# Moving the last up group of block two behind block four's out-projection, and giving the token forms other tiles

## The chip, the cores and the metric

One core of one Trainium2 chip runs the kernel: TensorE (PE) multiplies matrices into PSUM, VectorE (DVE) and ScalarE (ACT) compute between SBUF and PSUM, GpSimd (POOL) and SyncE (SP) issue DMAs here, POOL also small steps. The metric is the device time of one execution in microseconds, the median of several runs.

## The reference, cut to what matters

```python
# h: 2064 tokens x 1024 (16 meta tokens, then 2048), all float32
hn = rms_norm(h, g_mix); proj = hn @ w_in            # q, k, v and the Fourier input u
attn = block_attention(rope(q), rope(k), v)          # 4 heads, 2 key/value heads
four = fourier_mix(u, w_f)
h = h + concat(rms_norm(attn), rms_norm(four)) @ w_out
m = rms_norm(h, g_mlp)
h = h + jnp.square(jax.nn.relu(m @ w_up)) @ w_down   # 1024 -> 4096 -> 1024
return rms_norm(h, g_final)[:, N_META:]
```

The change lies between the end of attention and the end of the MLP.

## The kernel before

Products in float32 are made of three matmuls (`mm3`, lines 71 to 76): each operand is split into a high part (an ACT copy to fp32r, line 64) and a low part (a DVE subtraction, line 65).

The 2048 tokens form four blocks of 512, each with four row tiles of 128. Attention is a generator of steps (`attention`, line 662: 32 units of ten steps), run inside the MLP of earlier blocks: `mix` (line 883) advances another generator and, after each piece of it, attention to a share of its steps. `out_a(b)` (line 906) is the out-projection of block b, `up` and `down` (lines 965, 994) are one group of 512 hidden columns of the MLP: `up` leaves relu-squared activations, split, and `down` multiplies them with the down weights in two halves of the output columns. Weights come through `wtile` (line 874): three raw tiles `wr`, four `wh`, four `wl`.

Blocks one and two (b = 0, 1) run this MLP. `head(0)` and `head(1)` (line 1043) are mixed with attention (lines 1070 to 1075). In `head(1)` all groups but the last are done, up and down. Then, without attention, come `up(1, 7)`, `out_a(3)`, and `down(1, 7)`.

Blocks three and four share their MLP as one product of 1024 tokens by Strassen-Winograd, with seven products in the order "1265734" per group of columns (line 1088). `flip` (line 1128) transposes the normed rows of a block on PE and ACT into `b11`, `b21` (block three, read back from DRAM into `h2`) and `b12`, `b22` (block four). `b_form` (line 1149) splits one of the seven token forms, computed from these by `minus` (line 1178), into `bf` tiles. `up_weights` (line 1095) loads 1024 KB blocks `R0`, `R1` of the up weights and splits the seven weight forms, four ahead. The products go to PSUM banks `ux` and `uy`, from which ACT and DVE make copies `p` and results `c`, `s`; the results go out to DRAM (`s_d`). Tiles of a new pool take the places of tiles of released pools, and each may be written as soon as the tiles that had its place are done (`reuse_waits="tile"`).

The order in program text: `down(1, 7)` half 0 with the flips between, forms 1 and 2, `down(1, 7)` half 1, `final(1)` (line 1024: the last norm of block two, its rows out), then forms 6, 5, 7, 3 and 4. The program's builder may reorder instructions of an engine within what the data allow.

The down stage (`down_operands`, line 1301) forms both operands of its seven products per group from `s_d` and the down weights. Its first product's operands are made early in the up stage's tiles (`first_down`, line 1218); the weight block `w11`, read there into the place of `R1`, is used again for the first difference `t1` (lines 1343 to 1351). Raw activations have a ring of 6 (`ar`), split ones of 10 (`a`); split weights get their pool `dr` in the place of `sp` (lines 1422 to 1426). In the first group these loads are on POOL's queue, later on SP's.

Of the kernel before, what the change touches and what calls it, by code (L numbers as in the profile page):

```python
# [18 lines left out]
P = 128  # L19
# [110 lines left out]
def encoder_block(ctx: ExitStack, tc: tile.TileContext, x, meta, w_in, w_f,  # L130
# [768 lines left out]

    mp = Lines(tc.alloc_tile_pool(name="mp", bufs=1, reuse_waits="tile"), small)  # L900
# [5 lines left out]
    def out_a(b):  # L906
# [111 lines left out]
    def load_gfin(b):  # L1018
        gfin = [a_tile(f"gfin_{b}_{i}") for i in range(2)]
# [4 lines left out]
    def final(b, early=None):  # L1024

        b0, n = BLOCKS[b]
        hs = H.pop(b)
        gfin = early or load_gfin(b)
        for t in range(2 * n):
# [40 lines left out]
    n0, n1 = 8 + 4 + 8 * 15 + 8, 8 + 8 * 14 + 8  # L1070
# [7 lines left out]
    drain(up(1, 7))  # L1078
# [14 lines left out]
    hm = Lines(tc.alloc_tile_pool(name="hm", bufs=1, side="right", reuse_waits="tile"), small)  # L1093
# [31 lines left out]
    UW = up_weights()  # L1125
    ready = [next(UW) for _ in range(4)]

# [18 lines left out]
    b11, b21 = (ra.tile([P, 4, 512], F32, name=f"b{i}1", tag=f"b{i}1") for i in (1, 2))  # L1146
    BF = {}

    def b_form(name, t, src):
        t = t.rearrange("p l k n -> p (l k) n")  # L1150
        BF[name] = hi, lo = t[:, 0:4], t[:, 4:8]
        for c in (slice(0, 2), slice(2, 4)):
            split(hi[:, c], lo[:, c], src[:, c])

    B = {}

    def flips():
        yield from flip(2, h2, (b11, b21))
        hm.release()
        B["rb"] = rb = Lines(tc.alloc_tile_pool(name="rb", bufs=1, side="right", reuse_waits="tile"), small)  # L1160
        B["b"] = [rb.tile([P, 4, 512], F32, name=f"b{i}2", tag=f"b{i}2") for i in (1, 2, 3)]
        yield from flip(3, H.pop(3), B["b"][:2])
# [8 lines left out]
    b_form("1", ey.tile([P, 2, 4, 512], R32, name="bf1", tag="e0"), b11)  # L1171
    b_form("2", ey.tile([P, 2, 4, 512], R32, name="bf2", tag="e1"), b21)
# [3 lines left out]
    two = (slice(0, 2), slice(2, 4))  # L1176

    def minus(dst, a, b):
        for c in two:
            nc.vector.tensor_tensor(dst[:, c], a[:, c], b[:, c], op=ALU.subtract)  # L1180
# [12 lines left out]
    b_form("3", bt["3"], b22)  # L1193
# [3 lines left out]
    b_form("4", sl4.tile([P, 2, 4, 512], R32, name="bf4", tag="bf4"), b21)  # L1197
# [20 lines left out]
    def first_down():  # L1218
# [15 lines left out]
        yield w  # L1234

    first = first_down()
    for g in range(8):
# [5 lines left out]
        for name in ORDER:  # L1243
            hi, lo = ready.pop(0)
            m = BF[name]
            for p in range(2):
# [6 lines left out]
                for k in range(4):  # L1253
                    mm3(nc, o, (hi[:, k, ps], lo[:, k, ps]), (m[0][:, k], m[1][:, k]),
# [38 lines left out]
    *_, w11 = first  # L1293
    pc.release()
    sl4.release()
    sl.release()
    dn = Lines(tc.alloc_tile_pool(name="dn", bufs=1, reuse_waits="tile"), small)

    RING = {"a": (dn, 10)}

    def down_operands():

        for g in range(4):
# [11 lines left out]
            def stationary(name):  # L1315
                S[name] = []
                for h in range(2):
                    r = dn.tile([P, 2, 512], F32, name=f"a{name}_{g}_{h}", tag="ar", bufs=6)
                    eng = nc.sync if g else nc.gpsimd
                    eng.dma_start(r, s_d[g][:, ORDER.index(name), 2 * h:2 * h + 2])  # L1320
                    S[name].append(r)

            def form(name, src):
                got = []
                for h in range(2):
                    for x, r in (("a", S[name][h]), ("b", src[h])):
                        pool, bufs = RING[x]
                        own = x == "b" and name == "2"
                        hi, lo = (pool.tile([P, 2, 512], R32, name=f"{x}{e}{name}_{g}_{h}",
                                            tag=f"{x}{e}{h}" if own else x, bufs=1 if own else bufs) for e in "hl")  # L1330
# [218 lines left out]
```

## Time and profile before

| | us |
|---|---|
| median of 3 runs | 2378.97 |
| lowest, highest | 2374.52, 2379.42 |
| the profiled execution | 2378.81 |
| its span, first to last instruction | 2377.0 |
| PE busy | 2319.6 (98%) |
| DVE busy | 1751.8 (74%) |
| ACT busy | 1296.6 (55%) |

The profile is of one execution. The stages by time: input projections to about 310, Fourier part with attention to about 600, MLP of blocks one and two with attention to about 1660, the passage described above to 1737, the Strassen up stage to 2053, the down stage to the end. Busy time of PE is modelled at its end, so the time in which PE starts nothing is read from what it waited for.

### The profile page before, as it was taken

To read this page: it belongs to the slowest core of one execution; us is meant where nothing else is said; L and a number is where in the kernel's file an instruction comes from. 1 tells how busy PE (TensorE), PEld (TensorE's weight loads), DVE (VectorE), ACT (ScalarE), POOL (GpSimd) and SP (SyncE) were. 2 spreads that over 40 slices of the span, in tenths; PEclk is the share of its full clock that TensorE was granted. 3 is DMA by queue.
4 is the path that set the end of the run, shared out by engine and by line. 5 is a ranking of instruction groups with operands and counts; after the bars stand their busy time and mean duration, and the time that the engine had idled before them with its cause. 6 is when DMAs were issued, how large, how long until landed. Compare 5 with 4: busy or idle time off the path is not lost.

```text
span 2377.0 us, 33687 instructions
## 1 busy us (share of the span) xinstructions
PE 2319.6 (98%) x12326; PEld 1975.7 (83%) x12326; DVE 1751.8 (74%) x2961; ACT 1296.6 (55%) x2525; POOL 170.2 (7%) x225
## 2 busy tenths in 40 slices
PE   8999999999999999999999999999989999899998
PEld 7889889888788888888878888888868888788886
DVE  5435678998688877787887887887675656687786
ACT  6434355654666656565765665665565555543343
POOL 1212120101100000000000000000000000100000
PEclk9999999999999999999999999999999999999999
DMA  6334152434333222234242434223424444855431
GB/s 210 105 102 117 45 170 53 154 125 143 129 92 115 76 76 70 77 103 118 72 142 76 146 92 129 67 76 111 155 89 168 137 165 155 318 173 169 141 124 71
DMA packets 168534, 288.64 MB, mean 121 GB/s; under 512 B 14144, under 2 KB 63008, under 8 KB 168240
## 3 DMA queue, kind: packets, MB, share of 16 engines
q1 hardware_dynamic: 145968, 246.90, 32.0%
q0 software_dynamic: 22400, 39.59, 6.0%
q8 instruction: 97, 1.59, 0.3%
q14 instruction: 69, 0.57, 0.1%
HBM read 216.93 MB, written 69.50 MB: 121 GB/s over the span
## 4 chain that ended last, share of the span: by engine, by line
PE 75%; DVE 5%; ACT 2%; DMA 2%; issue 1%; POOL 1%; SPq 0%; POOLq 0%; DVEq 0%; ACTq 0%
PE pdn L74 5%; PE pdn L75 5%; PE pdn L76 5%; PE pup L74 4%; PE pup L75 4%; PE pup L76 4%; PE s L74 2%; PE s L76 2%; PE s L75 2%; PE ux L74 2%; PE ux L76 2%; PE ux L75 2%; PE o L757 2%; PE dx L75 2%; PE dx L74 2%; PE dx L76 2%
## 5 line engine op out<-in xcount | busy, mean ns | idle before, releaser
L74 PE MATMUL pdn<-wh_dn,ah 128*128 128x512 f32 x512 | 202.4, 397 | 0.8 <-ACT wh_dn L64 0.7
L74 PE MATMUL pup<-mT,wh_up 128*128 128x512 f32 x512 | 202.0, 396 | 0.6 <-ACT mT L67 0.6
L76 PE MATMUL pup<-mT,wl_up 128*128 128x512 f32 x512 | 202.4, 398 | 0.0
L75 PE MATMUL pup<-mT,wh_up 128*128 128x512 f32 x512 | 202.1, 395 | 0.0
L75 PE MATMUL pdn<-wl_dn,ah 128*128 128x512 f32 x512 | 202.1, 395 | 0.0
L76 PE MATMUL pdn<-wh_dn,al 128*128 128x512 f32 x512 | 199.8, 393 | 0.0
L696 ACT COPY S<-s 128x512 f32<-128x512 f32 (+1 forms) x288 | 159.8, 559 | 60.6 <-PE s L76 42.0
L736 DVE TENSOR_TENSOR S<-S,mb 128x512 f32<-128x512 f32 (+1 forms) x288 | 185.5, 652 | 4.8 <-ACT mb L725 4.7
L741 ACT ACTIVATE S<-S 128x512 f32<-128x512 f32 (+1 forms) x264 | 155.6, 602 | 60.8 <-DVE S L736 59.7
L64 ACT CAST wh_up<-wr_up 128x512 fp32r<-128x512 f32 x128 | 79.3, 620 | 167.7 <-PE pdn L76 71.8
L74 PE MATMUL s<-q,kt 128*128 128x256 f32 (+1 forms) x544 | 158.7, 292 | 1.1 <-ACT S L696 1.1
L703 DVE TENSOR_TENSOR M<-M,S 128x512 f32<-128x512 f32 (+1 forms) x224 | 145.2, 648 | 14.8 <-ACT S L696 13.3
L76 PE MATMUL s<-q,kt 128*128 128x256 f32 (+1 forms) x544 | 154.7, 284 | 0.0
L65 DVE TENSOR_TENSOR wl_up<-wr_up,wh_up 128x512 fp32r<-128x512 f32 x128 | 87.5, 687 | 90.5 <-ACT wh_up L64 90.4
L75 PE MATMUL s<-q,kt 128*128 128x256 f32 (+1 forms) x544 | 154.2, 283 | 0.0
L64 ACT CAST wh_dn<-wr_dn 128x512 fp32r<-128x512 f32 x128 | 79.2, 619 | 100.5 <-PE pdn L76 54.6
L65 DVE TENSOR_TENSOR wl_dn<-wr_dn,wh_dn 128x512 fp32r<-128x512 f32 x128 | 87.8, 686 | 54.9 <-ACT wh_dn L64 54.0
L64 ACT CAST ah<-a 128x1024 fp32r<-128x1024 f32 x56 | 58.6, 1050 | 121.8 <-issue 67.1
L763 DVE TENSOR_TENSOR acc<-acc,S 128x512 f32<-128x512 f32 x168 | 114.9, 684 | 2.2 <-ACT S L741 2.1
L65 DVE TENSOR_TENSOR pl<-S,ph 128x512 fp32r<-128x512 f32 x168 | 114.3, 684 | 2.1 <-ACT ph L64 1.3
L74 PE MATMUL o<-ph,vt 128*128 128x256 f32 x384 | 111.2, 290 | 2.1 <-ACT ph L64 2.0
L74 PEld LDWEIGHTS s<-q,kt 128*128 128x128 f32 (+1 forms) x544 | 102.7, 189 | 11.6 <-ACT S L696 2.3
(311 smaller groups left out, 6814.6 us busy)
## 6 DMA issues: line engine op xcount, KB each, us to landing
wr_up<-in_w_up_dram SPq DMA_DIRECT2D x128, 256.0 KB, 2.8
wr_dn<-in_w_down_dram SPq DMA_DIRECT2D x128, 256.0 KB, 2.7
a<-s_d SPq DMA_DIRECT2D x42, 512.0 KB, 3.6
R<-in_w_up_dram SPq DMA_DIRECT2D x16, 1024.0 KB, 5.6
s_d<-s SPq DMA_DIRECT2D x64, 256.0 KB, 2.1
d<-in_w_down_dram SPq DMA_DIRECT2D x26, 512.0 KB, 4.6
s_d<-c SPq DMA_DIRECT2D x48, 256.0 KB, 2.3
h<-h_d SPq DMA_DIRECT2D x20, 512.0 KB, 5.9
```

The lines of the kernel that those rows point to most:

```text
L64: nc.scalar.copy(hi, src)
L65: nc.vector.tensor_tensor(lo, src, f32v(hi), op=ALU.subtract)
L74: nc.tensor.matmul(out, a[0], b[0], start=first, stop=False, skip_group_check=chain)
L75: nc.tensor.matmul(out, a[0], b[1], start=False, stop=False, skip_group_check=chain)
L76: nc.tensor.matmul(out, a[1], b[0], start=False, stop=last, skip_group_check=chain)
L696: nc.scalar.copy(S[:rows, :n], ps[:rows, :n])
L703: nc.vector.tensor_tensor(M[:rows, :n], M[:rows, :n], S[:rows], op=ALU.max)
L736: nc.vector.tensor_tensor(S, S, bc(s["mb"][:rows], [rows, n, 256]), op=ALU.subtract)
L741: nc.scalar.activation(p, S, AF.Exp, scale=ISQ)
L757: nc.tensor.matmul(s["O"], vt[t // 4][:, t % 4], p[:, e], start=t == 0, stop=False)
L763: nc.vector.tensor_tensor(acc, acc, p, op=ALU.add)
```

## The change

- Attention is spread over `head(1)` without the second last down product; `down(1, 6)` follows when attention has ended, then `out_a(3)`. `up(1, 7)` now comes behind `out_a(3)`, with the flips between its pieces, and both halves of `down(1, 7)` behind it.
- The row tiles `h` get a pool `hp` of their own. `h2` lies in the places of `R0` and `R1`; the up weights start behind the flips. `b12`, `b22` and a third block are there from the start.
- Token forms are lists of tiles: 1 and 2 in `ey` as before, 5 in block four's rows and 7 in block two's (`in_hp`), 6 in the `wh` and `wl` slots (`in_wp`), 3 and 4 in small pools. Form 5 comes between the two down halves, 6 right behind them, ahead of `final(1)`.
- `final(1)` no longer has `gfin` multiplied into the first half beforehand; it loads `gfin` into `wr` slots and does both halves on DVE.
- The copies `p` of the first column half lie in `wr` slots, three each.
- Down stage: the first group loads the block (1, 1) again instead of keeping `w11`; two weight blocks and stationary "6" load behind form 2; form 2 has tiles of its own for both operands; the rings are 8 and 5; `gfin` is loaded first, and squares go to two fixed tiles.

```diff
+    hp = Lines(tc.alloc_tile_pool(name="hp", bufs=1, reuse_waits="tile"), small)
     mp = Lines(tc.alloc_tile_pool(name="mp", bufs=1, reuse_waits="tile"), small)
...
-            h = mp.tile([P, D], F32, name=f"h_{b}_{t}", tag=f"h{int(b == 1)}", bufs=4)
+            h = hp.tile([P, D], F32, name=f"h_{b}_{t}", tag=f"h{int(b == 1)}", bufs=4)
...
-                if early and i == 0:
-                    nc.scalar.activation(v, v, AF.Copy, scale=rs)
-                else:
-                    nc.vector.scalar_tensor_tensor(v, v, rs, gfin[i], op0=ALU.mult, op1=ALU.mult)
+                nc.vector.scalar_tensor_tensor(v, v, rs, gfin[i], op0=ALU.mult, op1=ALU.mult)
...
-            if grp < 7:
+            if grp < 7 - b:
                 yield from down(b, grp)
...
-    n0, n1 = 8 + 4 + 8 * 15 + 8, 8 + 8 * 14 + 8
+    n0, n1 = 8 + 4 + 8 * 15 + 8, 8 + 8 * 13 + 8
...
-    drain(up(1, 7))
+    drain(down(1, 6))
     drain(out_a(3))
...
-    UW = up_weights()
-    ready = [next(UW) for _ in range(4)]
-
     def flip(b, hs, raw):
...
-    for t in range(4):
-        h = hm.tile([P, D], F32, name=f"h2_{t}", tag=f"h2_{t}")
-        nc.sync.dma_start(h, h_d[8 + t])
-        h2.append(h)
+    for i in range(2):
+        h = sp.tile([P, 2, D], F32, name=f"h2_{i}", tag=f"R{i}")
+        for t in range(2):
+            nc.sync.dma_start(h[:, t], h_d[8 + 2 * i + t])
+            h2.append(h[:, t])
...
+    def in_ey(e):
+        t = ey.tile([P, 2, 4, 512], R32, name=f"bf{e}", tag=f"e{e}").rearrange("p l k n -> p (l k) n")
+        return [t[:, 0:2], t[:, 2:4]], [t[:, 4:6], t[:, 6:8]]
+
+    def in_hp(e, name):
+        t = [hp.tile([P, 2, 512], R32, name=f"bf{name}_{i}", tag=f"h{e}", bufs=4) for i in range(4)]
+        return t[:2], t[2:]
+
+    def in_wp(name):
+        return tuple([wp.tile([P, 1, 512], R32, name=f"bf{e}{name}_{i}", tag="w" + e, bufs=4) for i in range(4)]
+                     for e in "hl")
...
-    for _ in down(1, 7, (0,)):
-        next(fl)
+    for _ in up(1, 7):
         next(fl, None)
     drain(fl)
-    rb, (b12, b22, b22t) = B["rb"], B["b"]
-    gfin = load_gfin(1)
...
-    for t in range(4):
-        nc.vector.tensor_tensor(H[1][t][:, :512], H[1][t][:, :512], gfin[0], op=ALU.mult)
-    drain(down(1, 7, (1,)))
...
+    UW = up_weights()
+    ready = [next(UW) for _ in range(4)]
+    b_form("1", in_ey(0), b11)
+    b_form("2", in_ey(1), b21)
+    drain(down(1, 7, (0,)))
     minus(b11, b12, b11)
     minus(b22t, b22, b11)
-    final(1, gfin)
+    b_form("5", in_hp(0, "5"), b11)
+    drain(down(1, 7, (1,)))
+    b_form("6", in_wp("6"), b22t)
     mp.release()
-    wp.release()
     sl = Lines(tc.alloc_tile_pool(name="sl", bufs=1, reuse_waits="tile"), small)
-    bt = {n: sl.tile([P, 2, 4, 512], R32, name="bf" + n, tag="bf" + n) for n in "6573"}
-    b_form("6", bt["6"], b22t)
-    b_form("5", bt["5"], b11)
+    final(1, load_gfin(1, [wp.tile([P, 512], F32, name=f"gfin_1_{i}", tag="wr", bufs=3) for i in range(2)]))
     minus(b12, b22, b12)
-    b_form("7", bt["7"], b12)
-    b_form("3", bt["3"], b22)
+    b_form("7", in_hp(1, "7"), b12)
+    b_form("3", in_pool(sl, "3"), b22)
     minus(b21, b21, b22t)
...
-                    d[p] = pc.tile([P, 512], F32, name=f"p{name}_{nm}", tag="p", bufs=6)
+                    d[p] = (pc if p else wp).tile([P, 512], F32, name=f"p{name}_{nm}", tag="p" if p else "wr", bufs=3)
...
-    RING = {"a": (dn, 10)}
+    RING = {"a": (dn, 8)}
...
-                    r = dn.tile([P, 2, 512], F32, name=f"a{name}_{g}_{h}", tag="ar", bufs=6)
+                    r = dn.tile([P, 2, 512], F32, name=f"a{name}_{g}_{h}", tag="ar", bufs=5)
...
-            else:
-                raw[1, 1] = [w11[:, 0:2], w11[:, 2:4]]
             stationary("2")
             load(2, 1)
-            load(1, 2)
-            load(2, 2)
-            stationary("6")
             if g == 0:
-                t1 = [dn.tile([P, 2, 512], F32, name=f"d11_0_{h}", tag="d11", bufs=2) for h in range(2)]
-                sub(t1, raw[1, 2], raw[1, 1])
+                own2("a")
+                load(1, 1)
+            if g:
+                load(1, 2)
+                load(2, 2)
+                stationary("6")
             yield form("1", raw[1, 1]) if g else FIRST
             yield form("2", raw[2, 1])
-            t3, t4 = raw[1, 2], raw[2, 1]
+            if g == 0:
+                load(1, 2)
+                load(2, 2)
+                stationary("6")
+            t1, t3, t4 = raw[1, 1], raw[1, 2], raw[2, 1]
...
-            if g:
-                t1 = raw[1, 1]
-                sub(t1, raw[1, 2], raw[1, 1])
+            sub(t1, raw[1, 2], raw[1, 1])
             sub(t2, raw[2, 2], t1)
```

## Rows read from the trace of the kernel before

**Rows 1.** The page, busy us, share of the span and instructions by engine.

```profile
PE 2319.6 (98%) x12326; PEld 1975.7 (83%) x12326; DVE 1751.8 (74%) x2961; ACT 1296.6 (55%) x2525; POOL 170.2 (7%) x225
```

**Rows 2.** What PE waited for: us in total, times, longest; whole run.

```profile
PE uy L74 <- ACT bf L64: 7.5, 2, 6.9
PE dy L75 <- DVE bl L65: 6.2, 1, 6.2
...
PE uy L75 <- DVE bf L65: 1.7, 1, 1.7
PE ux L74 <- ACT p L1268: 1.4, 1, 1.4
...
PE pmt L1136 <- DVE h L1132: 0.7, 1, 0.7
PE pdn L74 <- ACT wh_dn L64: 0.7, 1, 0.7
```

**Rows 3.** Stretches: length, then busy us by engine, clock, DMA share, GB/s.

```profile
1746.40:1753.30 6.90, 0.00 (x0) 0.00 (x0) 6.46 (x9) 5.05 (x7) 1.68 (x2) 0.77 0.78 289
1753.30:1760.25 6.95, 5.22 (x11) 3.68 (x12) 6.95 (x7) 5.32 (x6) 0.00 (x0) 0.50 0.50 165
```

**Rows 4.** Timeline of PE: start us, duration, instruction, times; the passage.

```profile
1734.67 0.39 PE L75 MATMUL uy<-bf,wuh 128*128 128x512 f32 x1
1734.90 0.39 PE L76 MATMUL uy<-bf,wul 128*128 128x512 f32 x1
...
1736.71 0.39 PE L76 MATMUL pdn<-wh_dn,al 128*128 128x512 f32 x1
...
1757.26 0.63 PE L74 MATMUL uy<-bf,wuh 128*128 128x512 f32 x1
1757.69 0.63 PE L75 MATMUL uy<-bf,wuh 128*128 128x512 f32 x1
```

**Rows 5.** Stretches as in rows 3, start of the down stage.

```profile
2053.00:2065.00 12.00, 12.00 (x54) 9.62 (x52) 4.96 (x8) 4.06 (x5) 0.00 (x0) 1.00 1.04 406
...
2071.30:2075.00 3.70, 3.70 (x10) 2.94 (x11) 3.70 (x4) 3.24 (x4) 0.08 (x1) 0.58 0.00 0
```

**Rows 6.** Groups by line and shape, 1703.3 to 1790: busy us, mean ns; idle before.

```profile
L65 DVE TENSOR_TENSOR bf<-b,bf 128x1024 fp32r<-128x1024 f32 x14 | 16.1, 1219 | 7.7 <-ACT bf L64 7.7
...
L1136 PE MATMUL pmt<-ident,h 128*128 128x128 f32 x64 | 9.0, 277 | 0.7 <-DVE h L1132 0.7
...
L1132 DVE TENSOR_SCALAR h<-h,rs_m 128x1024 f32<-128x1024 f32 x8 | 5.9, 749 | 2.7 <-DMA h_d<-h 2.3 <-DMA h<-h_d 0.4
...
L1040 DVE SCALAR_TENSOR_TENSOR h<-h,rs_m,gfin 128x512 f32<-128x512 f32 x4 | 2.8, 749 | 0.9 <-POOL rs_m L186 0.9
...
L1174 DVE TENSOR_TENSOR h<-h,gfin 128x512 f32<-128x512 f32 x4 | 2.5, 687 | 0.0
```

**Rows 7.** DMA issues, 1703 to 1765: size each, median us to landing.

```profile
out_dram<-h SPq DMA_DIRECT2D x8, 256.0 KB, 2.3
R<-in_w_up_dram SPq DMA_DIRECT2D x1, 1024.0 KB, 7.2
```

**Rows 8.** Timeline of ACT, columns as in rows 4: the first copies `p`.

```profile
1764.22 1.07 ACT L1268 COPY p<-ux 128x512 f32<-128x512 f32 x2
```

**Rows 9.** Stretches as in rows 3, the MLP with attention.

```profile
640.00:1190.00 550.00, 547.62 (x3050) 467.04 (x3048) 443.36 (x787) 349.26 (x679) 25.94 (x36) 1.00 0.30 87
1220.00:1660.00 440.00, 439.93 (x2407) 375.45 (x2406) 352.61 (x626) 271.45 (x517) 15.61 (x21) 1.00 0.32 98
...
670.00:700.00 30.00, 29.09 (x168) 25.00 (x167) 28.25 (x53) 23.85 (x47) 2.15 (x3) 1.00 0.45 130
```

**Rows 10.** Timeline of ACT, the down stage's first forms; in brackets idle before, releaser.

```profile
2068.98 1.05 ACT L64 CAST bh<-d 128x1024 fp32r<-128x1024 f32 x1 [11.38 <-DVE d L1337]
```

**Rows 11.** A stretch as in rows 3, inside the down stage.

```profile
2133.00:2144.00 11.00, 11.00 (x50) 9.12 (x49) 11.00 (x13) 3.90 (x4) 0.00 (x0) 1.00 0.36 107
```

More of the change, by code (lines that the diff above doesn't have):

```diff
@@ L1016, in down, with load_gfin @@
                                          accum_out=sums[t][:, half:half + 1])
-    def load_gfin(b):
-        gfin = [a_tile(f"gfin_{b}_{i}") for i in range(2)]
+    def load_gfin(b, tiles=None):
+        gfin = tiles or [a_tile(f"gfin_{b}_{i}") for i in range(2)]
         for i in range(2):
@@ L1022, in load_gfin, with final @@
         return gfin
-    def final(b, early=None):
+    def final(b, gfin=None):
         b0, n = BLOCKS[b]
         hs = H.pop(b)
-        gfin = early or load_gfin(b)
+        gfin = gfin or load_gfin(b)
         for t in range(2 * n):
@@ L1092, in encoder_block @@
     ra = Lines(tc.alloc_tile_pool(name="ra", bufs=1, side="right", reuse_waits="tile"), small)
-    hm = Lines(tc.alloc_tile_pool(name="hm", bufs=1, side="right", reuse_waits="tile"), small)
+    rb = Lines(tc.alloc_tile_pool(name="rb", bufs=1, side="right", reuse_waits="tile"), small)
     def up_weights():
@@ L1141, in encoder_block @@
     h2 = []
-    for t in range(4):
-        h = hm.tile([P, D], F32, name=f"h2_{t}", tag=f"h2_{t}")
-        nc.sync.dma_start(h, h_d[8 + t])
-        h2.append(h)
+    for i in range(2):
[3 more added lines that the diff above has]
+            h2.append(h[:, t])
     b11, b21 = (ra.tile([P, 4, 512], F32, name=f"b{i}1", tag=f"b{i}1") for i in (1, 2))
+    b12, b22, b22t = (rb.tile([P, 4, 512], F32, name=f"b{i}2", tag=f"b{i}2") for i in (1, 2, 3))
@@ L1147, in encoder_block, with b_form @@
     BF = {}
-    def b_form(name, t, src):
-        t = t.rearrange("p l k n -> p (l k) n")
-        BF[name] = hi, lo = t[:, 0:4], t[:, 4:8]
-        for c in (slice(0, 2), slice(2, 4)):
-            split(hi[:, c], lo[:, c], src[:, c])
-    B = {}
+    def b_form(name, tiles, src):
+        BF[name] = tuple([t[:, i] for t in half for i in range(t.shape[1])] for half in tiles)
+        k = 0
+        for hi, lo in zip(*tiles):
+            n = hi.shape[1]
+            split(hi, lo, src[:, k:k + n])
+            k += n
@@ new lines, in minus @@
+    def minus(dst, a, b):
+        for c in (slice(0, 2), slice(2, 4)):
+            nc.vector.tensor_tensor(dst[:, c], a[:, c], b[:, c], op=ALU.subtract)
+    def in_ey(e):
[7 more added lines that the diff above has]
+                     for e in "hl")
@@ L1157, in flips, with in_pool @@
+    def in_pool(pool, name):
+        t = pool.tile([P, 8, 512], R32, name="bf" + name, tag="bf" + name)
+        return [t[:, 0:2], t[:, 2:4]], [t[:, 4:6], t[:, 6:8]]
     def flips():
         yield from flip(2, h2, (b11, b21))
[L1159 to L1162, printed above, removed]
+        yield from flip(3, H.pop(3), (b12, b22))
@@ L1196, in encoder_block @@
     sl4 = Lines(tc.alloc_tile_pool(name="sl4", bufs=1, reuse_waits="tile"), small)
-    b_form("4", sl4.tile([P, 2, 4, 512], R32, name="bf4", tag="bf4"), b21)
+    b_form("4", in_pool(sl4, "4"), b21)
     ra.release()
@@ L1233, in first_down @@
                 yield
-        yield w
     first = first_down()
@@ L1291, in encoder_block @@
                         keep("7", p, s3)
-    *_, w11 = first
+    drain(first)
     pc.release()
@@ L1296, in encoder_block @@
     sl.release()
+    hp.release()
+    wp.release()
     dn = Lines(tc.alloc_tile_pool(name="dn", bufs=1, reuse_waits="tile"), small)
-    RING = {"a": (dn, 10)}
+    RING = {"a": (dn, 8)}
     def down_operands():
@@ L1321, in stationary, with own2 @@
                     S[name].append(r)
+            own = {}
+            def own2(x):
+                for h in range(2):
+                    own[x, h] = [RING[x][0].tile([P, 2, 512], R32, name=f"{x}{e}2_{g}_{h}", tag=f"{x}{e}{h}")
+                                 for e in "hl"]
             def form(name, src):
@@ L1326, in form @@
                     for x, r in (("a", S[name][h]), ("b", src[h])):
[L1327 to L1330, printed above, removed]
+                        if name == "2":
+                            if (x, h) not in own:
+                                own2(x)
+                            hi, lo = own[x, h]
+                        else:
+                            pool, bufs = RING[x]
+                            hi, lo = (pool.tile([P, 2, 512], R32, name=f"{x}{e}{name}_{g}_{h}", tag=x, bufs=bufs)
+                                      for e in "hl")
                         split(hi, lo, r)
@@ L1370, in down_operands @@
             yield form("4", t4)
+    gfin = [dn.tile([P, 512], F32, name=f"gf{i}", tag=f"gf{i}") for i in range(2)]
+    for i in range(2):
+        nc.sync.dma_start(gfin[i], g_fin[i * 512:(i + 1) * 512].rearrange("(o d) -> o d", o=1).broadcast_to([P, 512]))
+    junks = [dn.tile([P, 512], F32, name=f"ej{i}", tag=f"ej{i}") for i in range(2)]
     DO = down_operands()
@@ L1374, in encoder_block @@
     load_h(1)
-    gfin = [dn.tile([P, 512], F32, name=f"gf{i}", tag=f"gf{i}") for i in range(2)]
-    for i in range(2):
-        nc.sync.dma_start(gfin[i], g_fin[i * 512:(i + 1) * 512].rearrange("(o d) -> o d", o=1).broadcast_to([P, 512]))
     halves = (slice(0, 512), slice(512, 1024))
@@ L1382, in square @@
     def square(t, half):
-        junk = dn.tile([P, 512], F32, name=f"ej_{t}_{half}", tag="ej", bufs=2)
-        nc.scalar.activation(junk, hs[t][:, halves[half]], AF.Square, accum_out=sums[t][:, half:half + 1])
+        nc.scalar.activation(junks[t % 2], hs[t][:, halves[half]], AF.Square, accum_out=sums[t][:, half:half + 1])
     def store(t):
```

8 lines of the change are left out of this document (1 added, 7 removed).

## The prediction

> **What bounds the kernel now.** The page comes first: TensorE (PE) is busy for 2319.6 of 2377.0 us [rows 1], and no other engine comes near it. What can be won is therefore idle time of PE, and time in which PE runs slowly. The second view is the list of what PE waited for in the whole run [rows 2]. Two places carry most of what does not belong to the start of the kernel. The first is the passage from attention to the Strassen up stage: waits for the token forms (the split operands `bf`) of 7.5 and 1.7 us, for the copy `p` of 1.4, for the scaled rows of 0.7 and for a down weight of 0.7, together 12.0 us. The second is the start of the Strassen down stage, where product "2" waits 6.2 us for its weight operand `bl`.
>
> The third view, engine time by stretch, shows what follows a long stop. In 1746.40 to 1753.30 PE does nothing while VectorE (DVE) is busy for 6.46 of 6.90 us, and in the next stretch the granted clock is 0.50, which is 1.2 of 2.4 GHz [rows 3]. In the timeline the matmuls then start 0.43 us apart, and later 0.23 [rows 4]. The 11 matmuls of that stretch so cost 11 x 0.20 = 2.2 us. **The first passage loses 14.2 us.** At the second, 10 matmuls take 3.70 us [rows 5] where 10 x 0.23 = 2.3 would do: 1.4 us. **The second loses 7.6 us.** Both together: 21.8 us of 2377.
>
> **The change, part by part.** The matmuls are the same; only their order changes, so PE's sum stays.
>
> *The last up group moves behind `out_a(3)`.* Before, only the 96 matmuls of `down(1, 7)` lie between `out_a(3)` and the Strassen stage, 96 x 0.23 = 22 us. Now `up(1, 7)` lies there too: 44 us, with 64 transposes in both, 9 us more [rows 6]. In this time DVE and ScalarE (ACT) must make the rows of the tokens, forms 1, 2 and 5, and the first four weight forms. DVE's new list up to the last down matmul: 16 weight low parts x 0.69, 8 scalings x 0.75, 8 additions of out-projection and down x 0.7, 4 activation low parts x 0.69, 6 form low parts, 4 subtractions, 4 weight-form low parts and 2 sums x 1.22 (0.69 for 512 columns, 1.22 for 1024 [rows 6]): about 45 of 53 us. It fits. `down(1, 6)` takes the old place of `up(1, 7)` as cover for the end of attention, equally long.
>
> *Weight forms of the up stage start later.* `UW` moves behind the flips, since the h2 rows now lie in `R0` and `R1`. That puts two loads of 1024 KB on SP's queue that wait for transposes; behind them stand the down weights and `gfin`. A load lands 7.2 us after issue [rows 7], and 22 us of down matmuls cover it. I take 0.
>
> *Form tiles no longer wait for `final`.* Before, forms 6, 5, 7, 3 and 4 all stand behind `final(1)` on ACT and DVE, 10 x 1.22 us on DVE alone, and the copy `p` of product "1" comes only at 1764.22, 27 us after the last down matmul at 1736.71 [rows 4, 8]. After, form 5 has its own tiles in the freed rows of block four and is made between the two down halves; form 6 takes the weight slots `wh` and `wl` as `down(1, 7)` frees them; the copies of half 0 lie in `wr`. So the fourth product needs nothing new, and the first form needed from the last tiles is 6, 10.9 us after the last down matmul (two products of 24 x 0.23).
>
> *What stays late.* Four multiplications by `gfin` (0.69 each) go from DVE, but the four first halves of `final` come to it from ACT, 0.75 each [rows 6]: a wash. Form 7 lies in block two's own rows, so it must wait until `final` has written them and their eight output DMAs have landed, 2.3 us each [rows 7]; behind its ACT cast stand the copies `p` and the next weight casts. It is needed four products, 21.8 us, after the last down matmul. DVE has until then: 4 additions x 0.69, form 6's four low parts x 0.69, `final` 8 x 0.75 and small steps 1, one `minus` and form 7 (4 x 1.22), one weight form with its difference (2 x 1.22), two additions x 0.69: 21.2 us. That is as much as there is, with the DMA in the chain. Bounds: 0, and the 10.0 us that PE waited for `bf` and `p` in the old order [rows 2] plus 2.2 of slow clock. I take 3, nearer to 0, because DVE may order forms 3 and 4 behind it and had 27 us of such work before.
>
> *The seam from `up(1, 7)` to `down(1, 7)`* loses the attention that hid relu, square and split at other seams. The first quarter of the group ends 18 matmuls, 4 us, before the last one, and its chain is three ACT steps of some 0.6 (two copies of that width take 1.07 [rows 8]) and a subtraction of 0.69: 2.5 us. Bounds 0 and 2; I take 0.5.
>
> *Attention is denser.* Its 233 steps are spread over 260 instead of 268 pieces of PE work, 3% more per piece. DVE is busy for 443.36 of 550 and 352.61 of 440 us there, 80%, with PE idle for 2.4 and 0.1 us [rows 9]. Bounds: a gain of the 2.4, and a loss of 5 (five of the 33 windows of 30 us becoming like that of 670 to 700, which lost 0.91 us). I take 1.
>
> *Start of the down stage.* ACT's cast `bh` of form 2 waited 11.38 us for a subtraction on DVE that reads the tile whose place it takes [rows 10]. The change loads that weight block again into a tile of its own, frees `R1` with the first split, moves the subtraction behind forms 1 and 2, and gives form 2's activation half its own slots too. On POOL's queue two loads of 512 KB are added ahead, and four weight loads and stationary "6" move behind form 2. What is next late: form 6, needed two products (21.8 us) after the start. Its weight loads go out when the last up product has freed the tiles; 2.1 MB at 406 GB/s are 5 us, sharing with others I estimate 10. DVE's work in that time is 12 parts x 1.22 and 4 additions x 0.69, 17.4 us. I take 1 us, bounds 0 and 6.2. The loads come into a stretch in which the DMA share is 1.04 at 406 GB/s [rows 5]. The Trainium skill, page DMA: Bandwidth & Descriptors, section Issuing engines are not separate DMA queues, speaks against them: DMAs from any engine run on the same 16 engines, so POOL's queue hides no transfer time; by it the new 1.05 MB would put 2.6 us at 406 GB/s in front of other loads, and the sum would give 2365. The trace agrees that the share is full.
>
> *`gfin` loads and `load_h(1)`* change places on SP; the second rows are used at the fourth product, 33 us in. I take 0; uncovered, they cost a landing, 7 us. *Rings of 8 and 5* instead of 10 and 6: PE never waits in a stretch where DVE is busy for 11.00 of 11.00 us [rows 11], and "2" leaves the ring, so each form still has a whole product of 10.9 us. I take 0; upper bound 5, where the subtractions overload DVE by 1.6 us in each of three groups.
>
> **Sum.** 21.8 - 3 - 0.5 - 1 - 1 = 16.3 us. The profiled execution took 2378.81 us (span 2377.0), beside a median of 2378.97, so I need no shift: 2378.8 - 16.3 = **2362.5 us**.
>
> **The rivals.**
> 1. *The stop returns at form 7* (chance 0.15). For it: DVE's list fills the time to the deadline, and the output DMAs lie in the chain. Against: forms 5 and 6 are out of that chain. It gives back 10.0 + 2.2 instead of 3: 2371.7.
> 2. *The second stop stays* (0.07): form 2 no longer waits for the subtraction, but for another tile or for the full DMA engines. Gain kept at the first passage only: 2362.5 + 6.6 = 2369.
> 3. *The change does not do what it says* (0.06): instructions are ordered by the program's builder (a `uy` matmul stands ahead of the last of `pdn` [rows 4]), and it may leave the forms behind `final`. Both losses stay: 2379.
> 4. *Slower: DVE becomes the bound of attention* (0.08). The window of 670 to 700 has DVE at 28.25 of 30 us and PE idle for 0.91 [rows 9]. If 3% more attention brought all 33 windows there, 33 x 0.91 less the 2.5 idle now is 27 us: 2362.5 - 1 + 27 = 2388.5. It outweighs the gain from 22 windows on, and shows as slower from 27. Against: the mean share is 80%, and the moved group takes its own DVE work along.
>
> **How the numbers follow.** The forecast has 0.64, with its own range of 2355 (all 21.8 and attention's 2.4 won) to 2368. The range to hold 8 in 10 reaches over rivals 1 and 2: 2355 to 2372. About 0.2% (4.8 us) is what a measurement can tell from no change. Faster: 0.64, rival 2, and 0.11 of rival 1: 0.82. Same: the rest of rival 1 (0.04) and rival 3 (0.06): 0.10. Slower: 0.08.
>
> **What would show it.** Right: PE waits for `bf` and `p` under 4 us in all, no stretch at 0.50 clock near the passage, form 5 cast before the last down half ends, `dy` not waiting for `bl` by more than 1 us. Wrong: PE waiting for form 7 some 20 us after the last `pdn`; a new wait of `dx` in the first group for form 6; PE idle over 5 us between 640 and 1660; or waits of `pdn` for activations after the last `pup`.

## The result, and the profile after

The changed kernel takes 2364.32 us (median of 6 runs, 2363.06 to 2365.22), the kernel before 2376.40 (median of 6, 2374.01 to 2379.42): the ratio is 0.9948, 95% interval 0.9936 to 0.9961. That is faster by 12.1 us, or 0.5%; the forecast was 2362.5 in a range of 2355 to 2372. The profiled execution took 2365.18 us, span 2363.4. One execution of the kernel no_reload below took 9184.2 us; its time is the median of its other three.

The page of the changed kernel, busy us by engine; beside [rows 1], PE does the same work in 13.6 us less span:

```profile
PE 2319.9 (98%) x12326; PEld 1974.5 (84%) x12326; DVE 1749.8 (74%) x2963; ACT 1292.6 (55%) x2523; POOL 171.3 (7%) x227
```

What PE waited for in the changed kernel, whole run (us in total, times, longest):

```profile
PE dy L75 <- DVE bl L65: 2.1, 1, 2.1
...
PE pdn L74 <- ACT ah L64: 2.0, 1, 2.0
PE dx L74 <- ACT ah L64: 1.9, 1, 1.9
...
PE pdn L74 <- ACT r L988: 1.2, 1, 1.2
...
PE ux L75 <- DVE bf L65: 0.8, 1, 0.8
PE uy L74 <- ACT bf L64: 0.6, 1, 0.6
...
PE ux L74 <- ACT p L1271: 0.2, 1, 0.2
```

Set against [rows 2], the passage's 12.0 us of waits have become 4.8: 1.0 of `ux` for a form and `p`, and 3.8 at the seam from `up(1, 7)` to `down(1, 7)` (`pdn` for `ah` and `r`, `uy` for a form). The 6.2 us of `dy` have become 2.1, but `dx`, product "6", now waits 1.9.

Three points of the trace divide the run: the starts of the last matmul of the out-projection (`poa`), of the up stage (`ux`) and of the down stage (`dx`). The moved group is 96 x 0.227 = 21.8 us of matmuls, so the changed kernel's first figure has 21.8 added and its second 21.8 taken off. One execution of each kernel:

| kernel | time, us (median) | `poa` | `poa` to `ux` | `ux` to `dx` |
|---|---|---|---|---|
| before | 2376.40 | 1703.0 | 350.1 | 312.6 |
| changed | 2364.32 | 1699.9 | 341.7 | 310.9 |
| before without its two losses | | 1703.0 | 335.9 | 305.0 |

The last row takes the 14.2 and the 7.6 us of the prediction off. So of 14.2 us the passage won 8.4, and of 7.6 the down stage won 1.7; the attention stage, which was to lose 1, won 3.1; the end won 0.4. Together 13.6 us, the difference of the spans. These parts are those of single executions: in four more kernels below whose passage is the changed kernel's (after_a1_210, adds_behind, no_reload, ahead), `poa` to `ux` takes 339.1 to 340.2 us instead of 341.7.

**The seam.** PE in the changed kernel's timeline (start us, duration, instruction, times, idle before and what ended it), and then the stretch behind it (length, busy us by engine, clock, DMA share, GB/s):

```profile
1710.86 0.51 PE L74 MATMUL pdn<-wh_dn,ah 128*128 128x512 f32 x1 [2.02 <-ACT ah L64]
1714.71 0.73 PE L74 MATMUL uy<-bf,wuh 128*128 128x512 f32 x2 [0.61 <-ACT bf L64]
1716.67 0.50 PE L74 MATMUL pdn<-wh_dn,ah 128*128 128x512 f32 x1 [1.23 <-ACT r L988]
```

```profile
1717.00:1720.00 3.00, 3.00 (x9) 2.36 (x8) 3.00 (x5) 3.00 (x6) 0.00 (x0) 0.56 0.04 7
```

3.86 us of idle time, then 9 matmuls in 3.00 us at 0.56 of the clock, which at 0.227 us each is 1.0 more: 4.8 us. ACT's timeline at the same place shows why:

```profile
1706.62 1.06 ACT L64 CAST wuh<-us 128x1024 fp32r<-128x1024 f32 x1
1707.55 0.65 ACT L989 ACTIVATE r<-r 128x512 f32<-128x512 f32 x1
1708.08 1.05 ACT L64 CAST wuh<-us 128x1024 fp32r<-128x1024 f32 x1
1709.02 1.28 ACT L1131 ACTIVATE b<-pmt,cols 128x512 f32<-128x512 f32 x2
1710.17 0.64 ACT L64 CAST ah<-r 128x512 fp32r<-128x512 f32 x1
```

Between the square of one quarter (L989) and its cast `ah` stand a weight cast and two copies of turned token rows, work of the next stage: 1.97 us, about the 2.02 that PE waits.

**The start of the down stage.** DVE in the changed kernel:

```profile
2050.23 0.69 DVE L1435 TENSOR_TENSOR hs<-hs,dx 128x512 f32<-128x512 f32 x1 [2.03 <-PE dx L76]
2050.84 1.22 DVE L65 TENSOR_TENSOR al<-a,ah 128x1024 fp32r<-128x1024 f32 x1
2052.95 0.69 DVE L1435 TENSOR_TENSOR hs<-hs,dx 128x512 f32<-128x512 f32 x1 [0.90 <-PE dx L76]
2053.56 1.22 DVE L65 TENSOR_TENSOR al<-a,ah 128x1024 fp32r<-128x1024 f32 x1
2054.69 2.36 DVE L65 TENSOR_TENSOR bl<-d,bh 128x1024 fp32r<-128x1024 f32 x2
```

Form 2's low parts have their data: ACT made the last `bh` by 2047.11, and no longer waits the 11.38 us of [rows 10]. But they stand behind additions (L1435) that wait for PE to finish a tile of product "1". The same holds for product "6": the first subtraction for its form (L1354) stands behind an addition that waits for product "2".

```profile
2059.24 0.69 DVE L1435 TENSOR_TENSOR hs<-hs,dy 128x512 f32<-128x512 f32 x1 [2.20 <-PE dy L76]
2059.85 1.22 DVE L1354 TENSOR_TENSOR d<-d,d 128x1024 f32<-128x1024 f32 x1
```

**The attention stage.** The stretch in which the two heads meet, in the kernel before and then in the changed one:

```profile
1170.00:1240.00 70.00, 65.34 (x366) 55.75 (x365) 62.10 (x114) 53.22 (x113) 3.99 (x5) 0.98 0.38 124
```

```profile
1170.00:1240.00 70.00, 69.50 (x393) 58.88 (x393) 61.41 (x113) 54.30 (x115) 3.60 (x5) 1.00 0.43 138
```

4.66 us of idle time have become 0.50, and 27 more matmuls fit.

### The profile page after: what moved, and what is told of

Same layout as the page of the kernel before. It is cut to its first block, busy times and chain, and to the rows that moved or that the text cites. A ratio compares the mean times of both kernels' runs of the same rounds, so it can differ in the third digit from the quotient of the medians.

```text
span 2363.4 us, 33659 instructions
## 1 busy us (share of the span) xinstructions
PE 2319.9 (98%) x12326; PEld 1974.5 (84%) x12326; DVE 1749.8 (74%) x2963; ACT 1292.6 (55%) x2523; POOL 171.3 (7%) x227
## 4 chain that ended last, share of the span: by engine, by line
PE 78%; DVE 4%; ACT 2%; DMA 2%; issue 1%; POOL 1%; DVEq 0%; POOLq 0%; ACTq 0%; SPq 0%
PE pdn L74 5%; PE pdn L75 5%; PE pdn L76 5%; PE pup L75 4%; PE pup L74 4%; PE pup L76 4%; PE s L74 2%; PE s L76 2%; PE s L75 2%; PE ux L74 2%; PE ux L76 2%; PE ux L75 2%; PE o L757 2%; PE dx L75 2%; PE dx L74 2%; PE dx L76 2%
## 5 line engine op out<-in xcount | busy, mean ns | idle before, releaser
L703 DVE TENSOR_TENSOR M<-M,S 128x512 f32<-128x512 f32 (+1 forms) x224 | 145.3, 649 | 13.4 <-ACT S L696 12.1
L74 PEld LDWEIGHTS pdn<-wh_dn,ah 128*128 128x128 f32 x512 | 97.1, 190 | 21.9 <-ACT r L988 2.6
L76 PEld LDWEIGHTS pdn<-wh_dn,al 128*128 128x128 f32 x512 | 96.3, 188 | 20.1 <-DVE al L65 0.4
```

The costliest lines, as they stand in the source:

```text
L74: nc.tensor.matmul(out, a[0], b[0], start=first, stop=False, skip_group_check=chain)
L76: nc.tensor.matmul(out, a[1], b[0], start=False, stop=last, skip_group_check=chain)
L703: nc.vector.tensor_tensor(M[:rows, :n], M[:rows, :n], S[:rows], op=ALU.max)
```

## The experiments

The columns are those of the table above (kernels that move the group: 21.8 added and taken off). Ratios to the kernel before, with 95% intervals, come from runs on the same chip. The kernels ahead and flip2 are adds_behind with one more edit, and early2 is flip2 with one more; before_a1_214 is the kernel before with one edit, and the rest are the changed kernel with one. Diffs are cut at the dots.

| kernel | us | ratio | `poa` | to `ux` | to `dx` |
|---|---|---|---|---|---|
| before_a1_214 | 2372.63 | 0.9979 [0.9970, 0.9989] | 1698.2 | 349.0 | 312.1 |
| after_a1_210 | 2367.16 | 0.9959 [0.9944, 0.9974] | 1701.6 | 339.1 | 312.5 |
| tiles_only | 2367.32 | 0.9957 [0.9940, 0.9973] | 1700.9 | 344.2 | 312.4 |
| forms_behind | 2363.66 | 0.9945 [0.9930, 0.9960] | 1697.1 | 342.7 | 310.9 |
| seam_behind | 2367.53 | 0.9963 [0.9948, 0.9977] | 1699.0 | 344.4 | 312.5 |
| adds_behind | 2359.07 | 0.9931 [0.9915, 0.9948] | 1696.3 | 339.9 | 306.9 |
| no_reload | 2357.22 | 0.9923 [0.9907, 0.9940] | 1695.3 | 340.1 | 307.1 |
| ahead | 2359.45 | 0.9923 [0.9908, 0.9938] | 1695.9 | 340.2 | 307.3 |
| flip2 | 2352.60 | 0.9897 [0.9882, 0.9912] | 1697.2 | 334.9 | 306.9 |
| early2 | 2354.63 | 0.9909 [0.9892, 0.9925] | 1696.7 | 336.3 | 308.5 |

The eight kernels with the changed kernel's attention order (it and seven others) end that stage between 1695.3 and 1699.9, so a single execution says nothing of 4 us there; the medians and the stops in the trace do.

### Where the attention stage won

Dropping one piece from `head(1)` lowers `n1`, and `a1`, the step at which the second head begins, goes from 210 to 214. Two kernels change that number alone.

```diff
-    a1 = a0 + (a2 - a0) * n0 // (n0 + n1)
+    a1 = 214
```

> The kernel before with one number changed: the attention steps are shared out so that the second block's head begins at step 214 and not 210, as they are in the changed kernel, because the piece that leaves head(1) shortens its count. Theory: the 3 to 4 us by which the attention stage ended earlier than forecast come from this: in the kernel before, TensorE waits 2.0, 0.7 and 2.0 us between 1190 and 1217, where the two heads meet, and falls to 0.94 of its clock behind it; with step 214 the stretch 1100 to 1300 goes from 195.3 us of work to about 199.5, and the time falls to 2372 to 2374 us. Rival: the stretch is better because head(1) has one piece less; then the stop at 1190 to 1217 stays and the time is 2376 us.

> The changed kernel with the one number set back: the second head begins at attention step 210. Theory: the stop where the heads meet comes back (two waits of about 2 us and a lower granted clock behind them), the stretch 1100 to 1300 falls from 199.5 to 200 us of work to about 195.5, and the time rises by 3 to 4 us to 2367 to 2368 us. Rival: the share-out doesn't matter: 2364 us and no stop.

Both came as the theory had it. The kernel before with 214 takes 4.8 us less than the kernel before of the same runs (2377.40), the interval clear of 1. The changed kernel with 210 takes 2.8 us more than the changed kernel, but these two come from different runs and their intervals overlap, so here it is the returned stop that counts. The stretch of the stop in the kernel before with 214, and what PE waited for in that stretch in the changed kernel with 210:

```profile
1170.00:1240.00 70.00, 70.00 (x398) 60.16 (x397) 60.94 (x112) 53.34 (x113) 3.31 (x5) 1.00 0.42 141
```

```profile
PE o L74 <- ACT ph L64: 2.0, 1, 2.0
PE pup L76 <- DVE wl_up L65: 0.9, 1, 0.9
PE pd_m L709 <- DVE mx L722: 0.8, 1, 0.8
PE s L74 <- ACT S L696: 0.5, 1, 0.5
```

The stop goes with the number in both kernels. So by the medians 3 to 5 of the change's 12 us come from a share-out that shifted along, and can be had in the kernel before by one integer.

### The two parts of the passage, each by itself

> The changed kernel's tiles and forms with the order of groups of the kernel before: up(1,7) ahead of the out-projection, the token tiles of block four turned beside down(1,7), two pieces at a step, and forms 1 and 2 behind the first half of down(1,7). It tells what the tiles earn without the moved group. Theory by the run with forms 5 and 6 put back on the old queue, which lost only about 1 us: the moved group is what gives the forms their time, so the passage stops again here, for 6 to 10 us with the half-clock stretch behind it, though form 5's tiles no longer wait: from the last out-projection to the last up product, less the 28.1 us of the moved group, it takes 343 to 347 us instead of 335.4, and the time is 2371 to 2375 us. Rival: the tiles alone let forms 5 and 6 start ahead of block two's last step, and that is enough: 2364 to 2367 us.

```diff
-            if grp < 7 - b:
+            if grp < 7:
 ...
-    n0, n1 = 8 + 4 + 8 * 15 + 8, 8 + 8 * 13 + 8
+    n0, n1 = 8 + 4 + 8 * 15 + 8, 8 + 8 * 14 + 8
 ...
-    drain(down(1, 6))
+    drain(up(1, 7))
 ...
-    for _ in up(1, 7):
+    for _ in down(1, 7, (0,)):
+        next(fl, None)
         next(fl, None)
 ...
-    drain(down(1, 7, (0,)))
```

The expectation took 28.1 us off the changed kernel's passage, the time from the last `poa` to the last `pup`. That holds most of the 64 transposes, which this kernel has too. The figures to set 344.2 against are 341.7 and, with `a1` at 210 as here, 339.1. The stop is there, for a weight form and not for a token form. ACT in this kernel, and what PE waited for:

```profile
1743.86 1.05 ACT L64 CAST bf<-b 128x1024 fp32r<-128x1024 f32 x1 [4.01 <-DMA out_dram<-h]
1748.07 0.59 ACT L1271 COPY p<-ux 128x512 f32<-128x512 f32 x1 [3.16 <-DVE h L1037]
...
1753.23 1.99 ACT L64 CAST bf<-b 128x1024 fp32r<-128x1024 f32 x2 [2.76 <-DVE bf L65]
1755.13 1.04 ACT L64 CAST wuh<-R 128x1024 fp32r<-128x1024 f32 x1
```

```profile
PE ux L74 <- ACT wuh L64: 6.4, 1, 6.4
```

A form's cast waits for an output DMA of block two's rows, the next copy for `final` (L1037), two more casts for a form's low part, and the weight cast stands behind them all. PE stops for 6.4 us, then runs at 0.50 of the clock in 1756 to 1760. This is the first rival of the prediction, with its queue; it appears when the moved group doesn't give DVE and ACT the time. Yet the time is 2367.32: without the group, `a1` is 210, and the changed kernel at 210 takes 2367.16. At equal `a1` the medians differ by 0.2 us, and the intervals are 3.9 and 3.6 us wide to either side; the two profiled executions, of which this kernel's (2370.31) was its slowest, differ by 3.4, and their passages by 5.1. So these runs leave the move of the group, once the tiles are there, between nothing and some 5 us.

> The changed kernel with forms 5 and 6 of block four put back behind block two's final steps on VectorE; the order of the groups and the tiles stay as changed. Theory: of the passage's 12 us idle before the change most was this queue: TensorE stops again for its forms at 1741 and later, 5 to 9 us of idle time and 1 to 2 us at half clock behind it, 2370 to 2374 us. Rival: the moved up group alone gives the forms time enough, and the queue on VectorE no longer matters: under 2 us, 2364 to 2366 us.

```diff
-    b_form("5", in_hp(0, "5"), b11)
     drain(down(1, 7, (1,)))
-    b_form("6", in_wp("6"), b22t)
 ...
+    with tc.issue_after(LASTF[0]):
+        b_form("5", in_hp(0, "5"), b11)
+        b_form("6", in_wp("6"), b22t)
```

The rival was right. The time is the changed kernel's, and the passage is longer than its 341.7 by 1.0 us, with one wait for a form:

```profile
PE uy L75 <- DVE bf L65: 2.6, 1, 2.6
```

The edit holds back forms 5 and 6 on DVE alone, their low parts; ACT cast form 6's high parts from 1727.75 on, ahead of `final`. Against all five passages of the changed kernel's code (339.1 to 341.7), low parts ahead of `final` are worth 1.0 to 3.6 us once the group gives the time, of which the medians show nothing. Without the group the tiles still win 5.9 of the passage's 8.4 us. The two overlap. The moved group on the old tiles was not run.

### The seam

> The changed kernel with block four's first four weight forms and its forms 1 and 2 issued behind the last high part (ah) of block two's last up group; the same work, another order on ScalarE. Theory: the idle time of TensorE at the seam between up(1,7) and down(1,7) (2.02, 0.61 and 1.23 us, and about 1 us more at half clock behind them) comes from ScalarE, busy without a gap from 1706 to 1720, where casts of the next stage stand between the steps of the up group's own chain; with these casts behind the chain, 3 to 4 of the 4.9 us go, the last multiplication of the up stage (ux, 2041.6) starts 3 to 4 us earlier, and the time is 2360 to 2362 us. Rival: the chain of copy, square, cast for four tiles is itself as long as the wait, or the casts are then late for the up products of block four and the wait only moves there: 2364 us, with new waits of uy or ux on bf or wuh behind the seam.

```diff
+    chain = ins_of(split.hi)
+    with tc.issue_after(chain):
-    UW = up_weights()
+        UW = up_weights()
 ...
```

The rival was right, and it cost 2.7 us in the passage instead of gaining. No `pdn` waits any more, but behind the seam:

```profile
PE ux L74 <- ACT p L1273: 3.9, 3, 2.1
PE uy L75 <- DVE bf L65: 2.6, 2, 1.6
```

This other order of the same work between 1700 and 1760 only moves the wait. Stretches of the kernel adds_behind (below), whose passage has the changed kernel's program, show where there is room, and those of flip2 what became of it:

```profile
1680.00:1690.00 10.00, 10.00 (x58) 8.52 (x57) 3.55 (x6) 5.38 (x9) 0.10 (x1) 1.00 0.42 138
1690.00:1700.00 10.00, 10.00 (x57) 8.49 (x56) 4.04 (x5) 6.57 (x11) 0.00 (x0) 1.00 0.79 275
1700.00:1710.00 10.00, 8.40 (x39) 6.38 (x38) 9.80 (x10) 9.97 (x16) 0.00 (x0) 0.93 0.05 15
1710.00:1720.00 10.00, 9.46 (x38) 7.16 (x37) 10.00 (x13) 7.59 (x13) 0.00 (x0) 0.90 0.16 53
```

```profile
1690.00:1700.00 10.00, 10.00 (x54) 8.49 (x53) 8.20 (x8) 8.64 (x12) 0.00 (x0) 1.00 0.41 145
1700.00:1710.00 10.00, 9.93 (x44) 7.92 (x43) 8.42 (x11) 9.20 (x15) 0.00 (x0) 1.00 0.24 79
1710.00:1720.00 10.00, 10.00 (x46) 8.26 (x45) 10.00 (x13) 8.32 (x17) 0.00 (x0) 1.00 0.09 28
```

In 1680 to 1700 DVE (third busy figure) works 7.59 of 20 us, in 1700 to 1720 19.80 of 20. In flip2 4 us of its work stand before 1700.

> The kernel with the additions behind form 2's low parts (2359.07 us), and besides two pieces of block four's token turning, not one, at each step of block two's last up group. Theory of the seam after the two runs on it: the waits of 1.6 to 2.0, 0.5 to 1.2 and 0.6 us between up(1,7) and down(1,7) come from more work of ScalarE and VectorE than the 1700 to 1720 stretch holds (VectorE 9.80 and 10.00 of 10 us, ScalarE 9.97 and 7.59), which is why putting the casts behind the up chain only moved the wait; VectorE is at 3.55 and 4.04 of 10 us in 1680 to 1700, so work moved there costs nothing. With the flips done earlier the weight tiles come free and are split some 5 us earlier, the waits fall to under 1 us together, from the last out-projection to the last up product it takes 359 to 360.5 us instead of 361.7, and the time is 2356.5 to 2358 us. Rival: the up chain (copy, square, cast four times) is the wait whatever stands between, since it can't start before the last up product: 361.7 us and 2359 us.

```diff
     for _ in up(1, 7):
         next(fl, None)
+        next(fl, None)
```

The theory was right, and the gain larger than it said: the seam's waits are gone, the clock stays at 1.00, and the passage takes 334.9 us, 5.0 less than in adds_behind and as short as the kernel before without its losses. 2352.60 us is 23.7 under the kernel before of the same runs (2376.26), about twice what the change won; it is the fastest kernel of this study.

> The same with two pieces at a step, and block four's first four weight forms and its forms 1 and 2 issued within up(1,7), behind its third step, not behind it. Theory: as for the kernel with two pieces alone, and the casts of forms 1 and 2 may now stand ahead of the up chain's third and fourth tile on ScalarE, four casts of 1.08 us: if they do, a wait of pdn on ah or r of up to 2 us stays. The time is then 2357 to 2360 us. Rival: the earlier casts free the stretch behind the seam, where VectorE is at 9.81 of 10 us in 1720 to 1730, and the time is 2355 to 2356.5 us.

```diff
-    for _ in up(1, 7):
+    for step, _ in enumerate(up(1, 7)):
 ...
+        if step == 2:
+            UW = up_weights()
+            ready = [next(UW) for _ in range(4)]
+            b_form("1", in_ey(0), b11)
+            b_form("2", in_ey(1), b21)
 ...
-    UW = up_weights()
-    ready = [next(UW) for _ in range(4)]
-    b_form("1", in_ey(0), b11)
-    b_form("2", in_ey(1), b21)
```

2354.63 us, with waits of 0.4 and 0.7 us at the seam (`uy` for a form, `pdn` for `r`): the theory's place, a third of its upper size. The time lies under both forecasts, 2357 to 2360 and the rival's 2355 to 2356.5, and the interval overlaps flip2's. So no run shows that an earlier place in the text brings anything more once the room before 1700 is used.

### The start of the down stage

> The changed kernel with the last three of the four additions to the token tiles of down product 1 issued behind the low parts of form 2 on VectorE. Theory: the wait of dy on bl at the start of the down stage (2.15 us at 2055.97) comes from form 2's low parts that stand behind these additions, which wait for TensorE; with them ahead the wait goes, the last dx starts 1 to 2 us earlier and the time is 2362 to 2363 us, if the wait of product 6 on its form (1.88 us, and 1 us at half clock) doesn't grow. Rival: form 6 ends when its data have come and been subtracted, whatever product 2 does; then product 6 waits so much longer (about 4 us instead of 1.88) and the time stays at 2364 us.

```diff
 ...
+                    two = ins_of(split.last)
 ...
+                    with ExitStack() as behind:
+                        if g == 0 and name == "1" and t:
+                            behind.enter_context(tc.issue_after(two))
-                    add(t)
+                        add(t)
```

The wait of `dy` is gone, and product "6" didn't take it over: it still waits 1.88 us, at 2060.17 instead of 2068.11. Its form is made earlier too. DVE in this kernel:

```profile
2051.31 0.69 DVE L1435 TENSOR_TENSOR hs<-hs,dy 128x512 f32<-128x512 f32 x1 [3.17 <-PE dy L76]
2051.91 1.22 DVE L1354 TENSOR_TENSOR d<-d,d 128x1024 f32<-128x1024 f32 x1
```

From this first addition of product "2" to the start of product "6" it takes 8.86 us, and 8.87 in the changed kernel (2059.24 to 2068.11): its subtractions stand right behind that addition, and product "6" moves with it. `ux` to `dx` falls by 4.0 us, about twice the wait, since no half-clock stretch follows either. The profiled execution (2355.72) was the quickest of this kernel. Its median is 5.3 under the changed kernel's, its ratio 0.0017 (4.0 us) under, and the two intervals overlap.

> The changed kernel without the second load of the down weights' block (1,1) in the first group: the first difference takes block (2,1) in its place, so the 1.05 MB are not moved and the values of that product differ; the counts of instructions on the engines are the same. Theory: the loads of blocks (1,2) and (2,2) queue behind 1.05 MB at some 400 GB/s, land about 2.5 us earlier without it, and product 6's wait on its form (1.88 us at 2068.1, then about 1 us at half clock) goes by 2 to 3 us: 2361 to 2362 us. Rival: the wait is VectorE's and ScalarE's order (subtractions, low parts, the b half cast ahead of the a half), not the load: product 6 waits as before, 2364 us.

```diff
-                load(1, 1)
 ...
+            if g == 0:
+                raw[1, 1] = [dn.tile([P, 2, 512], F32, name=f"d11_0_{h}", tag="d11", bufs=2) for h in range(2)]
 ...
-            sub(t1, raw[1, 2], raw[1, 1])
+            sub(t1, raw[1, 2], raw[1, 1] if g else raw[2, 1])
```

The kernel leaves out the load and subtracts another block in its place. Here the other wait goes: `dy` waits 2.15 us for `bl` as before, `dx` for nothing, and `ux` to `dx` is 307.1. But the edit changed the order on DVE as well: the first two subtractions now stand ahead of the additions of product "2".

```profile
2050.73 2.35 DVE L1354 TENSOR_TENSOR d<-d,d 128x1024 f32<-128x1024 f32 x2
2053.05 0.69 DVE L1436 TENSOR_TENSOR hs<-hs,dy 128x512 f32<-128x512 f32 x1
```

DMA stretches of the changed kernel and of this one, in which the first `dy` starts at 2052.8 and 2046.5:

```profile
2060.00:2062.00 2.00, 2.00 (x11) 1.65 (x10) 1.78 (x3) 0.00 (x0) 0.00 (x0) 1.00 0.58 226
```

```profile
2052.00:2054.00 2.00, 2.00 (x11) 1.64 (x10) 2.00 (x3) 0.00 (x0) 0.00 (x0) 1.00 0.26 107
```

The share is 1.03 to 1.07 up to these stretches, and 0.58 and 0.26 of 2 us are 1.2 and 0.5. So the engines are full until 8.4 us behind the first `dy` with the reload, and 6.0 without it: 2.4 us for 1.05 MB. The prediction weighed this by the Trainium skill, page DMA: Bandwidth & Descriptors, section Issuing engines are not separate DMA queues: DMAs run on the same 16 engines, whichever engine starts them. The trace agrees that the loads on POOL's queue keep these engines full for longer, and the prediction's estimate of 2.6 us was the right size.

Whether these 2.4 us reached PE is not shown. Product "6" can have been freed by the earlier loads or by the new order on DVE; the equal 8.86 and 8.87 us above speak for the order. A kernel with the reload and with the subtractions ahead of the additions was not run.

> The kernel with the additions behind form 2's low parts, and besides form 6 of the down stage's first group in another order: both high parts of its stationary (ah) ahead of those of its moving operand (bh) on ScalarE, and its low parts in the order bl, bl, al, al on VectorE. Theory: of the one wait left there (1.88 us of dx on ah, at 2060.17 in the run before) ScalarE's order holds all but 0.3 to 0.5 us, since the stationary has landed 2 us before bh is made: the wait falls to about 0.5 us, and from the last up product to the last down product it takes 305.4 us instead of 306.9; the time is 2357.5 to 2358 us. Rival: low parts then come late and the wait moves to al or bl: 307 us from product to product, 2359 us.

```diff
+                    for hi, lo, r in got[::2] + got[1::2]:
 ...
+                            ins = ins_of(nc.scalar.copy(hi, r))
 ...
+                    for hi, lo, r in got[1::2] + got[::2]:
 ...
+                            split.last = nc.vector.tensor_tensor(lo, r, f32v(hi), op=ALU.subtract)
```

Each step is issued behind the one ahead of it in this order, and two later subtractions (`t3`, `t4`) behind form 6's low parts. The rival was right: 2359.45 us, and `dx` no longer waits for `ah` but for the low parts.

```profile
PE dx L75 <- DVE bl L1363: 1.5, 1, 1.5
PE dx L76 <- DVE al L1363: 0.6, 1, 0.6
```

ACT's order was the last releaser in the profile and not the limit; DVE was, with additions, subtractions and low parts in a nearly unbroken row from product "2"'s first addition (2051.25) on. That addition had waited 3.16 us for PE.

## Why the prediction held, point by point

The terms, as forecast and as the profiled execution has them; they are what is left of the losses, or new:

| term | forecast, us | measured, us |
|---|---|---|
| form 7, with the copies behind `final` | 3 (0 to 12) | 1.0 |
| seam to `down(1, 7)` | 0.5 (0 to 2) | 4.8 |
| attention | 1 (-2.4 to 5) | -3.1 |
| start of the down stage | 1 (0 to 6.2) | 5.9 |
| end | 0 | -0.4 |
| sum | 5.5 | 8.2 |

The median came out 1.8 us above the forecast and the profiled execution 2.7: misses of 4.3 and 4.9 us at the seam and the down stage, and of 2.0, 4.1 and 0.4 on the other side. That they nearly cancel is luck: most of the 4.1 goes with `a1`, of which the prediction says nothing.

- **Passage: right.** That `final` and its DMAs held forms and copies, and that a wait there brings a half-clock stretch, is shown by tiles_only, in which a stop came back through that chain. In the changed kernel forms and `p` wait 1.0 us in all. The signs named ahead came out as said for forms and `p` (under 4 us), not for the clock (0.56 behind the seam) and not for `dy` (2.1 us, over 1); two of the signs of being wrong came, `pdn` waiting for activations (3.2 us) and `dx` for form 6 (1.9). That the passage needed the moved group, as the sum took for granted, is borne out for 2.5 us (341.7 against 344.2 in tiles_only) to 5.1 (339.1, at equal `a1`), and the medians don't show it.
- **The seam: the failing step; 4.8 us, over its own upper bound of 2.** I counted the three ACT steps of a quarter and took them as a chain. The trace has other work between them. I should have added up what DVE and ACT have to do from 1700 to 1720 and not only until the last down matmul: "45 of 53 us" fits as a sum, but DVE is full in those 20 us and not half busy in the 20 before. flip2 shows that starting this work earlier removes the waits, seam_behind that putting the next stage's casts behind the chain only moves them.
- **Attention: wrong sign.** I treated the 3% more attention per piece as the effect and passed over what else `n1` enters: `a1`. The stop at 1190 to 1217, the largest in that stage, was in the trace before, between the two windows of [rows 9], and I costed neither it nor its cause.
- **Down stage: mis-sized, inside its bounds.** The subtraction that held form 2 is gone, as said. I asked what form 6 would wait for, and bounded the rest by 6.2, but didn't look at DVE's order, where additions that wait for PE stand ahead of form 2's low parts and of form 6's subtractions. The two waits (2.15 and 1.88 us) and one half-clock stretch (1.6) make 5.6 of the 5.9; adds_behind and no_reload each remove one wait, adds_behind by DVE's order alone.
- **No charge for `gfin`, the rings and the weight loads: right** as far as a trace shows it; no wait of PE in the changed kernel's list names them. Rival 4, DVE as the bound of attention, didn't come: DVE's share there rose only from 443.36 [rows 9] to 447.27 of 550 us.

## What to carry to other kernels

When a deadline is met as a sum, check it in slices of 10 us: here an engine was at 4 of 10 before a seam and at 10 of 10 behind it, and PE waited there; one reordering of the full slice only moved the wait, and starting the work earlier removed it. Ask of each count that a change touches what else is derived from it; here one integer that moved along carried some 3 to 5 of the 12 us. When two parts of a change give time to the same queue, test each without the other before crediting either. And when an edit is to test a load, compare the order of the engines' instructions too: the program's builder may have changed it.

## What the runs showed of the hardware

A wait of PE of the same 1.9 to 2.15 us was followed by 1.2 GHz in some executions and not in others. With both waits of the down stage the changed kernel and forms_behind fell once (0.50 behind `dx`), and after_a1_210, seam_behind and tiles_only fell behind both; with the one wait of 2.15 us, no_reload stayed at 1.00; with the one wait of 1.88 us, adds_behind and flip2 stayed at 1.00, and early2, otherwise the same there, fell:

```profile
2059.00:2061.00 2.00, 2.00 (x6) 1.52 (x6) 2.00 (x2) 2.00 (x3) 1.06 (x2) 0.50 0.29 27
```

```profile
2058.00:2060.00 2.00, 2.00 (x11) 1.61 (x9) 2.00 (x2) 2.00 (x3) 1.01 (x2) 1.00 0.27 31
```

The first is early2, the second flip2. A fall costs 1.6 us: in the changed kernel 8 matmuls from 2068.91 to 2072.32 take 3.41 where 1.82 would do, and `ux` to `dx` steps by that much, 306.9 and 308.5 with one wait, 310.9 and 312.5 with two. I had charged half-clock stretches only to the long stops; a 2 us wait is worth up to 3.6 us. These are executions of different kernels, one profile each, so whether the difference between executions of one kernel comes from such falls is not shown, nor why one execution falls and another doesn't.
